# Regrouping 32-row blocks through DRAM instead of within SBUF, and another order of the first pair's loads and splits

## The chip, the cores and the metric

The kernel runs on one core of one Trainium2 chip. The metric is the time of one execution on the device in microseconds, the median of several runs. The engines are called as in the profile: PE is TensorE (matmuls; PEld its weight loads), DVE is VectorE, ACT is ScalarE, POOL is GpSimd, SP is SyncE, which here only issues DMAs.

## The reference

One layer of a hybrid encoder on x of 1 x 512 x 1024 in float32: an RMS norm, one wide input projection, two token mixers, a gated merge, an output projection and the residual.

```python
h = rmsnorm(x, norm_w)
proj = einsum('bsd,de->bse', h, w_in) + b_in
(mq, mk, mv, mi, mf, mo, mz, sq, sk, sv, sz, gates) = split(proj)
# A) mLSTM, 4 heads of 256, on conv+silu of mq, mk; y_m = rmsnorm(hm) * sigmoid(mo) * silu(mz)
# B) stick-breaking attention, 8 heads of 128, strictly causal:
#    A[t,s] = sigmoid(z_ts) * prod_{s<j<t} (1 - sigmoid(z_tj));  y_s = (A v) * silu(sz)
merged = g_m * (y_m @ w_proj_m) + g_s * (y_s @ w_proj_s)
out = x + merged @ w_out
```

## The kernel before

Every float32 operand of a matmul is split into a high and a low half in the matmul's own type (`wh` and `wl` for weights: a copy on ACT, a subtraction on DVE, or, where a unit is marked `by_dma`, a negated copy on ACT and an accumulating DMA issued by POOL), and each product is three matmuls (lines 94 to 96).

The dense work is a list of units, and the main loop runs over them: in step c it moves the result of unit c-1 out of PSUM (`evac`), runs what is due in step c (`later`; `defer(n, fn)` puts something n steps ahead), loads and splits the weights of the units ahead, issues the first half of unit c's matmuls, lets each active attention head take one step of its generator (up to its next `yield`), and issues the second half. In the steps of `REST` the heads do not advance. All of this is an order written by hand; each engine works through its own queue strictly in that order. A tile has a tag with a fixed number of buffers; a new tile waits until its buffer's last readers have finished. Tag A has four buffers, which the `ay`, `a_all` and `ty` tiles, `hz`, the first pair's `X` and `Y` and the token blocks of x share.

Units 0 to 3 make the first attention set's q (`first_mm`). Units 4 to 17 and 18 to 31 are two Strassen pairs (`Pair`, `Half`): seven products of two half units each instead of eight, with sums of the quarters of the weights (`X`, `Z`, `V`, `Y`, made by `t1` to `t4`; `t3` adds V to Y by a DMA of POOL) and of the quarters of h (`form_sum` on DVE over the copies `h32`, which `x_32` makes on ACT; `form_split` splits them on ACT and DVE). Half units take half the time of the later units. From unit E = 32 on come z of set 0, q, k and z of set 1, and then the gates and the mLSTM groups. The heads of set 0 and set 1 (`SbSet.head`) and the four mLSTM heads (`MPair.head`) run beside them.

Three places turn a matrix of 128-column blocks round. VectorE transposes 32 x 32 blocks, and DMAs then regroup blocks of 32 rows:
- `SbSet.turn` writes q or k transposed in blocks to `ty`; `move`, one step later, regroups it into `tz` by 16 DMAs of 32 KB, eight on SP's queue and eight on POOL's (line 441); `weight` then scales `tz` for q.
- `SbSet.head` writes the attention weights in blocks to `ay` and regroups them into `az` by 16 DMAs of 40 KB on SP's queue, eight in one step and eight in the next (line 542); `turn` splits `az` into `ath` and `atl` some steps later.
- `MPair.head` regroups `ht` into `hz` by 16 DMAs of 32 KB on SP's queue (line 874).

Of the kernel before, what the change touches and what calls it, by code (L numbers as in the profile page):

```python
# [8 lines left out]
F32 = mybir.dt.float32  # L9
# [28 lines left out]
def tile_hybrid_layer(  # L38
# [16 lines left out]
    nc = tc.nc  # L55
# [3 lines left out]
    def pool(name, bufs=1, **k):  # L59
        return ctx.enter_context(tc.tile_pool(name=name, bufs=bufs, **k))  # L60
# [6 lines left out]
    dp = pool("dp", space=bass.MemoryType.DRAM)  # L67
# [9 lines left out]
    def blk(tag, dt=F32, shape=(512,), name=None, p=128):  # L77

        where = mp if tag in MISC else sp
        return where.tile([p] + list(shape), dt, name=name or tag, tag=tag, bufs=BUFS[tag])  # L80
# [51 lines left out]
    units = []  # L132
# [72 lines left out]
    def defer(n, fn):  # L205
        later.setdefault(now[0] + n, []).append(fn)
# [78 lines left out]
    def x_scale(tb):  # L285
        x_norm(tb)
        x_mul(tb)
# [16 lines left out]
    def x_mul(tb):  # L304
        nc.vector.tensor_scalar(x_t[tb], x_t[tb], x_r[tb], None, op0=OP.mult)
# [3 lines left out]
    def x_tp(tb, g):  # L309
        tp = x_ps[tb, g] = att_ps()  # L310
        for j in range(4):
            kt = g * 4 + j
            nc.tensor.transpose(tp[:, j * 128:(j + 1) * 128], x_t[tb][:, kt * 128:(kt + 1) * 128], ident)

    def x_hh(tb, g):
        ks = slice(4 * g, 4 * g + 4)
        nc.vector.tensor_tensor(hh[:, ks, tb * 128:(tb + 1) * 128],
                                x_ps[tb, g].rearrange("p (k t) -> p k t", k=4),
                                nw_t[:, ks].unsqueeze(2).to_broadcast([128, 4, 128]), op=OP.mult)

    def x_hl(tb, *ks):
        ts = slice(tb * 128, (tb + 1) * 128)
        for k in ks:
            tp = x_ps[tb, k // 4][:, k % 4 * 128:k % 4 * 128 + 128]
            nc.vector.scalar_tensor_tensor(hl[:, k, ts], tp, nw_t[:, k:k + 1],
                                           hh[:, k, ts].bitcast(F32), op0=OP.mult, op1=OP.subtract)
# [3 lines left out]
    def x_32(tb, g):  # L330
        for k in range(4 * g, 4 * g + 4):
            at = tb // 2, k // 2
            if not at in h32:
                t = blk("vl", name="h32") if len(h32) < 5 else blk("vh", shape=(576,), name="h32")[:, 0:512]
                h32[at] = t.rearrange("p (k t) -> p k t", k=2)
            c = 128 * (tb % 2)
            nc.scalar.activation(h32[at][:, k % 2, c:c + 128], x_ps[tb, g][:, k % 4 * 128:k % 4 * 128 + 128],
                                 AF.Copy, scale=nw_t[:, k:k + 1])

    def x_turn(tb):  # L340
        for g in range(2):
            x_tp(tb, g)
            x_hh(tb, g)
            x_hl(tb, *range(4 * g, 4 * g + 4))
            if tb > 1:
                x_32(tb, g)
# [11 lines left out]
    class SbSet:  # L358
# [66 lines left out]
        def turn(self, name, g):  # L425

            ty = sp.tile([128, 8, TB, 32], F32, name="ty", tag="A", bufs=4)
            for tb in range(TB):  # L430
                nc.vector.transpose(ty[:, :, tb, :],  # L431
                                    self.raw[name][tb][:, 256 * g:256 * g + 256].rearrange("p (x j) -> p x j", j=32))

            def move():
                tz = blk("qk", F32, (2, 4, 128), name="tz")
                self.tz[name, g] = tz
                src = ty.rearrange("p (h b) i j -> p b h (i j)", h=2)
                for b in range(4):
                    for a in range(4):
                        q = nc.gpsimd if a % 2 else nc.sync  # L440
                        q.dma_start(tz[32 * b:32 * b + 32, :, a, :], src[32 * a:32 * a + 32, b])  # L441

            def weight():
                z = self.tz[name, g]
                nc.vector.tensor_scalar(z, z, qkw, None, op0=OP.mult)

            defer(1, move)
            if name == "q":
                defer(3 if self.s else 6, weight)
            if name == "q" and g == 0:  # L450
                defer(2, lambda: self.turn(name, 1))

# [11 lines left out]
        def head(self, h):  # L464
# [55 lines left out]
            ay = sp.tile([128, 4, 10, 32], F32, name="ay", tag="A", bufs=4)  # L520
# [16 lines left out]
                blocks(i)  # L537
            yield
            az = sp.tile([128, 4, 10, 32], F32, name="az", tag="P5", bufs=2)
            for b in range(4):  # L540
                for a in range(4):
                    nc.sync.dma_start(az[32 * a:32 * a + 32, b, :, :], ay[32 * b:32 * b + 32, a, :, :])  # L542
                if b == 1:
                    yield
            yield
            yield
            while not ("v", self.s) in done:
# [141 lines left out]
    class MPair:  # L689
# [85 lines left out]
        def head(self, h):  # L775
# [15 lines left out]
            for j in range(TB):  # L791
                lo = j * 128
                w = w_all[:, P_OFF[j]:P_OFF[j] + T - lo]
                for i in range(j, TB):
                    s = slice((i - j) * 128, (i - j + 1) * 128)
                    src = w[:, s] if i == j else rbc[:, i * 128:(i + 1) * 128]
# [53 lines left out]
            ht = sp.tile([128, 8, TB, 32], F32, name="ht", tag="A", bufs=4)  # L850
# [17 lines left out]
            turn(3)  # L868
            yield
            hz = sp.tile([128, 2, T], F32, name="hz", tag="A", bufs=4)  # L870
            src = ht.rearrange("p (d a) i j -> p a d (i j)", d=2)
            for a in range(4):
                for b in range(4):
                    nc.sync.dma_start(hz[32 * a:32 * a + 32, :, 128 * b:128 * b + 128],
                                      src[32 * b:32 * b + 32, a])
            yield
            yield
            for d in range(2):
                y = y_m[2 * hd + d].rearrange("p (i b j) -> p i b j", i=TB, b=4)
# [28 lines left out]
    def h_form(row, col):  # L908
        def sta(k, tb):
            c = slice(256 * row + 128 * tb, 256 * row + 128 * tb + 128)  # L910
            return hh[:, 4 * col + k, c], hl[:, 4 * col + k, c]
        return sta
# [49 lines left out]
    class Pair:  # L962

        def __init__(self, c1, c2, got1, got2):
            self.c = {1: c1, 2: c2}
            self.got = {1: got1, 2: got2}
            self.raw, self.bank, self.dst = {}, {}, {}
            self.sta = {1: h_form(0, 0), 2: h_form(0, 1), 6: s_form(6), 5: s_form(5),
                        7: s_form(7), 3: s_form(3), 4: h_form(1, 1)}
            b = self.base = len(units)  # L970
            for p in (1, 2, 6, 5, 7, 3, 4):
                for g in range(2):
                    units.append(Half(self, p, g))
            first = b == 4
            for g in range(2):
                if first:
                    plan = {"X": g, "Z": g, "V": g, "Y": 1}
                else:
                    plan = {"X": b - 8 + g, "Z": b - 8 + 6 * g, "V": b - 4 + g, "Y": b - 6 + g}
                for name, c in plan.items():  # L980
                    self.at(c, self.load, name, g)
                self.at(b + g - 2, self.t3, g)
                self.at(b + 1 + g, self.t2, g)
                self.at(b + 3 + g, self.t4, g)
                self.at(b + 4 + g, self.t1, g)
            self.at(b + 1, self.rows)

        def at(self, c, fn, *a):
# [75 lines left out]
    def at_unit(c, fn, *a):  # L1064
        later.setdefault(c, []).append(lambda: fn(*a))

    for g in range(2):
        at_unit(1 + g, units[4 + g].split)
    for f in (5, 7, 6):
        for i in range(2):  # L1070
            at_unit(2, form_sum, f, i)
    for f, c in ((6, 3), (5, 5), (7, 7), (3, 9)):
        for i in range(2):
            at_unit(c + i, form_split, f, i)
    for i in range(2):
        at_unit(8, form_sum, 3, i)

# [418 lines left out]
    for c in range(N):  # L1496
        now[0] = c
        if 0 < c < TB:
            ahead(c)
        if c and units[c - 1].slow:  # L1500
            units[c - 1].slow()
            ahead(c)
        due = later.pop(c, [])
        if c > n_proj - 9:
            ahead(c)
        if c:
            units[c - 1].evac()
        for fn in due:
            fn()
        ahead(c)  # L1510
        units[c].mm(0)
        if c == 0:
            x_tp(1, 0)
            x_tp(1, 1)
            x_hh(1, 0)
            x_hl(1, 0, 1, 2, 3)
            x_norm(2)
            x_mul(2)
            x_hh(1, 1)
            x_hl(1, 4, 5, 6, 7)  # L1520
            x_scale(3)
            for n in range(4):
                x_32(n // 2, n % 2)
        if c == 1:
            x_turn(2)
        for g in list(act):
            if c in REST:
                continue
            if next(g, "end") == "end":
                act.remove(g)  # L1530
        for e in list(pend):
            if c >= e[0] and e[2]():
                pend.remove(e)
                g = e[3]()
                next(g)
                act.append(g)
        units[c].mm(1)
        if c == 1:
            x_turn(3)
# [31 lines left out]
```

## Time and profile before

| | |
|---|---|
| median of 3 runs | 706.59 us (706.04 to 706.91) |
| profiled execution | 707.75 us, of which the span of its trace is 706.0 us |
| PE busy | 678.5 us, 96% |
| DVE, ACT, POOL busy | 490.1, 375.6, 151.8 us |
| mean granted clock of TensorE | 0.987 of full speed |
| moved by DMA | 101.52 MB, of which HBM read 69.37 MB, written 5.30 MB |
| issues for `az`, `hz`, `tz` | 128 and 64 on SP; 48 on SP and 48 on POOL |

A row of the timeline gives the start in us, the time taken, engine, line, operation, output and inputs by the program's names, and in square brackets how long the engine had been idle before it and what ended that. SPq and POOLq rows are issues of DMAs. A row with "x8" merges eight instructions that follow each other. A group's row gives its count, then busy time and the mean of one in ns, then the idle time before them. A row of DMA issues gives count, size and, for POOL, the median time from issue to landing.

### The profile page before, as it was taken

The page shows a single profiled execution, that of the slowest core. Times are in us where ns is not written, and L with a number is a line of the kernel's source. Part 1 is how long each engine was busy: PE and PEld are TensorE (multiplying, and loading weights), DVE is VectorE, ACT ScalarE, POOL GpSimd, SP SyncE. Part 2 cuts the span into 40 slices and gives each one's busy share as a digit, 9 for nine tenths or more (in the row PEclk, how much of TensorE's full clock was granted, in tenths as well). Part 3 has the DMA queues.
Part 4 walks back from the last instruction along what each step waited for, and adds up shares of the span by engine and source line. Part 5 has one row for each costly group of instructions (what it writes and reads, how often), then busy time and mean ns, then how long its engine had stood idle before and what let it go on. Part 6 is the DMA issues. An engine that isn't in the chain of part 4 may idle for free.

```text
span 706.0 us, 9541 instructions
## 1 busy us (share of the span) xinstructions
PE 678.5 (96%) x3114; PEld 562.3 (80%) x3114; DVE 490.1 (69%) x849; ACT 375.6 (53%) x705; POOL 151.8 (21%) x316
## 2 busy tenths in 40 slices
PE   7988999999949999999999999999999999999997
PEld 5876868888737888888887888888888888888786
DVE  6876687766466886698998446599733365545897
ACT  7656445765826554564445664444647452444361
POOL 4124327365634420130001031100001200111010
PEclk9998999999988999999999999999999999999999
DMA  7947947569643465525445414234332344989333
GB/s 244 303 101 208 234 132 180 143 163 221 154 120 103 107 188 178 156 57 144 102 97 146 134 60 120 77 104 133 106 103 70 90 123 139 307 189 225 112 78 102
DMA packets 128306, 101.52 MB, mean 144 GB/s; under 512 B 19786, under 2 KB 105188, under 8 KB 128256
## 3 DMA queue, kind: packets, MB, share of 16 engines
q1 hardware_dynamic: 121104, 83.48, 40.5%
q0 software_dynamic: 7008, 17.31, 12.8%
q8 instruction: 24, 0.39, 0.2%
q14 instruction: 26, 0.21, 0.1%
q10 hardware_dynamic: 144, 0.13, 0.1%
HBM read 69.37 MB, written 5.30 MB: 106 GB/s over the span
## 4 chain that ended last, share of the span: by engine, by line
PE 62%; DVE 9%; DMA 7%; issue 5%; ACT 4%; SPq 2%; POOL 0%; DVEq 0%; ACTq 0%; POOLq 0%
PE dps L96 17%; PE dps L94 17%; PE dps L95 17%; PE aps L95 2%; PE aps L96 2%; PE aps L94 2%; DMA wl<-stg 2%; DVE acc L724 2%; DMA stg<-in_w_in_dram 2%; DMA Y<-V 2%; SPq L542 2%; PE dps L955 2%; DVE wl L100 1%; PE aps L955 1%; DMA az<-ay 1%
## 5 line engine op out<-in xcount | busy, mean ns | idle before, releaser
L94 PE MATMUL dps<-hh,wh 128*128 128x512 f32 x448 | 176.5, 394 | 10.9 <-DVE kraw L387 10.4
L96 PE MATMUL dps<-hh,wl 128*128 128x512 f32 x448 | 175.4, 391 | 0.6 <-DVE wl L100 0.6
L95 PE MATMUL dps<-hl,wh 128*128 128x512 f32 x448 | 175.2, 391 | 0.0
L100 DVE TENSOR_TENSOR wl<-stg,wh 128x1024 fp32r<-128x1024 f32 x68 | 83.4, 1226 | 56.1 <-ACT wh L99 55.7
L94 PEld LDWEIGHTS dps<-hh,wh 128*128 128x128 f32 x448 | 84.7, 189 | 28.4 <-issue 10.8
L96 PEld LDWEIGHTS dps<-hh,wl 128*128 128x128 f32 x448 | 84.5, 189 | 19.1 <-DVE wl L100 1.1
L95 PEld LDWEIGHTS dps<-hl,wh 128*128 128x128 f32 x448 | 84.7, 189 | 16.8
L99 ACT ACTIVATE wh<-stg 128x1024 fp32r<-128x1024 f32 x68 | 71.6, 1052 | 29.4 <-PE dps L95 10.9
L506 DVE TENSOR_TENSOR_SCAN om<-om 128x512 f32<-128x512 f32 (+3 forms) x32 | 26.9, 839 | 19.3 <-POOL om L500 19.3
L94 PE MATMUL dps<-wh,hh 128*128 128x512 f32 x96 | 37.6, 392 | 1.3 <-DVE qraw L387 1.3
L727 ACT ACTIVATE tmp<-acc 128x512 f32<-128x512 f32 x16 | 10.1, 633 | 52.3 <-DVE acc L724 52.3
L95 PE MATMUL dps<-wl,hh 128*128 128x512 f32 x96 | 37.4, 390 | 0.0
L96 PE MATMUL dps<-wh,hl 128*128 128x512 f32 x96 | 37.4, 390 | 0.0
L724 DVE SCALAR_TENSOR_TENSOR acc<-tmp,vec,acc 128x511 f32<-128x511 f32 (+2 forms) x48 | 36.0, 750 | 1.7
L128 POOL DMA_DIRECT2D wl<-stg x16 | 14.3, 892 | 94.5 <-DVE yml L100 40.0
L126 ACT ACTIVATE wh<-stg 128x1024 fp32r<-128x1024 f32 x16 | 16.9, 1058 | 28.4 <-PE dps L95 16.9
L786 POOL TENSOR_SCALAR_AFFINE_SELECT w_all<-om 128x128 f32<-128x128 f32 x16 | 7.7, 514 | 108.3 <-DMA om<-rb_d 108.3
L441 POOL DMA_DIRECT2D tz<-ty x48 | 26.0, 570 | 12.7 <-DVE ty L431 6.6
L500 POOL TENSOR_SCALAR_AFFINE_SELECT om<-om 128x128 f32<-128x128 f32 x32 | 16.0, 506 | 58.3 <-ACT om L498 58.1
L96 PE MATMUL dps<-yh,wl 128*128 128x512 f32 x64 | 25.0, 391 | 0.6 <-DMA wl<-stg 0.6
L95 PE MATMUL dps<-yl,wh 128*128 128x512 f32 x64 | 24.9, 389 | 0.0
L94 PE MATMUL dps<-yh,wh 128*128 128x512 f32 x64 | 24.9, 389 | 0.0
(303 smaller groups left out, 1567.4 us busy)
## 6 DMA issues: line engine op xcount, KB each, us to landing
stg<-in_w_in_dram SPq DMA_DIRECT2D x71, 512.0 KB
wl<-stg POOLq DMA_DIRECT2D x16, 512.0 KB, 5.5
az<-ay SPq DMA_DIRECT2D x128, 40.0 KB
stg<-in_w_proj_s_dram SPq DMA_DIRECT2D x8, 512.0 KB
B<-in_w_out_dram SPq DMA_DIRECT2D x8, 512.0 KB
stg<-in_w_proj_m_dram SPq DMA_DIRECT2D x8, 512.0 KB
dst<-u POOLq DMA_DIRECT2D x12, 256.0 KB, 5.5
X<-in_w_in_dram SPq DMA_DIRECT2D x4, 512.0 KB
```

Of the source, the lines that this page charges most:

```text
L94: nc.tensor.matmul(ps, ah, bh, start=first, stop=False)
L95: nc.tensor.matmul(ps, ah, bl, start=False, stop=False)
L96: nc.tensor.matmul(ps, al, bh, start=False, stop=last)
L99: nc.scalar.activation(hi, src, AF.Copy)
L100: nc.vector.tensor_tensor(lo, src, hi.bitcast(F32), op=OP.subtract)
L126: nc.scalar.activation(self.wh, self.st, AF.Copy)
L128: nc.gpsimd.dma_start(out=self.wl, in_=self.st, accum_op=OP.add)
L441: q.dma_start(tz[32 * b:32 * b + 32, :, a, :], src[32 * a:32 * a + 32, b])
L500: nc.gpsimd.affine_select(out=om[:, ts], in_=om[:, ts], compare_op=OP.is_gt, fill=1.0, base=0, channel_multiplier=1, pattern=[[-1, 128]])
L506: nc.vector.tensor_tensor_scan(back, back, back, 1.0, op0=OP.mult, op1=OP.bypass)
L724: nc.vector.scalar_tensor_tensor(acc[:, j:], t[:, 0:T - j], cw(3 - j, ch), acc[:, j:], op0=OP.mult, op1=OP.add)
L955: nc.tensor.matmul(pr.bank[key, tb], a, w[:, i, :], start=begin and n == 0, stop=end and n == 2, skip_group_check=again)
```

## The change

The three regroupings go through a parking tile in DRAM. `tz`: four stores of 32 partitions each, and one step later (`back`) four loads, all on SP's queue; `weight` in set 1 moves from 3 to 4 steps after `turn`. `az`: one store of the whole `ay`, and one step later four loads. `hz`: four stores, and one step later four loads.

In the first pair, the eight weight loads go out as X0, Z0, V0 in step 0 and Y0, X1, V1, Y1, Z1 in step 1 (before, Z1 and V1 stood between X1 and Y1). The split of unit 5 moves from step 2 to step 1, behind the turning of token block 2 and ahead of that of block 3. The forms 5 and 7 are split one or two steps earlier.

```diff
             def move():
                 tz = blk("qk", F32, (2, 4, 128), name="tz")
                 self.tz[name, g] = tz
-                src = ty.rearrange("p (h b) i j -> p b h (i j)", h=2)
-                for b in range(4):
-                    for a in range(4):
-                        q = nc.gpsimd if a % 2 else nc.sync
-                        q.dma_start(tz[32 * b:32 * b + 32, :, a, :], src[32 * a:32 * a + 32, b])
+                park = dp.tile([32, 2, 4, 4, 128], F32, name="t_d", tag="t_d", bufs=3)
+                for a in range(4):
+                    nc.sync.dma_start(park[:, :, :, a].rearrange("i h b x -> i (h b) x"),
+                                      ty[32 * a:32 * a + 32].rearrange("i g n j -> i g (n j)"))
+
+                def back():
+                    for b in range(4):
+                        nc.sync.dma_start(tz[32 * b:32 * b + 32].rearrange("i h a x -> i h (a x)"),
+                                          park[:, :, b].rearrange("i h a x -> i h (a x)"))
+
+                defer(1, back)
...
             if name == "q":
-                defer(3 if self.s else 6, weight)
+                defer(4 if self.s else 6, weight)
...
             az = sp.tile([128, 4, 10, 32], F32, name="az", tag="P5", bufs=2)
-            for b in range(4):
-                for a in range(4):
-                    nc.sync.dma_start(az[32 * a:32 * a + 32, b, :, :], ay[32 * b:32 * b + 32, a, :, :])
-                if b == 1:
-                    yield
+            park = dp.tile([4, 32, 4, 320], F32, name="a_d", tag="a_d", bufs=3)
+            nc.sync.dma_start(park.rearrange("b i a x -> (b i) (a x)"), ay.rearrange("p a n j -> p (a n j)"))
+            yield
+            for a in range(4):
+                nc.sync.dma_start(az[32 * a:32 * a + 32].rearrange("i b n j -> i b (n j)"),
+                                  park[:, :, a].rearrange("b i x -> i b x"))
             yield
             yield
...
             hz = sp.tile([128, 2, T], F32, name="hz", tag="A", bufs=4)
-            src = ht.rearrange("p (d a) i j -> p a d (i j)", d=2)
+            park = dp.tile([32, 2, 4, 4, 128], F32, name="h_d", tag="h_d", bufs=2)
+            for b in range(4):
+                nc.sync.dma_start(park[:, :, :, b].rearrange("i d a x -> i (d a) x"),
+                                  ht[32 * b:32 * b + 32].rearrange("i g n j -> i g (n j)"))
+            yield
             for a in range(4):
-                for b in range(4):
-                    nc.sync.dma_start(hz[32 * a:32 * a + 32, :, 128 * b:128 * b + 128],
-                                      src[32 * b:32 * b + 32, a])
-            yield
+                nc.sync.dma_start(hz[32 * a:32 * a + 32], park[:, :, a].rearrange("i d b x -> i d (b x)"))
             yield
...
             first = b == 4
             for g in range(2):
-                if first:
-                    plan = {"X": g, "Z": g, "V": g, "Y": 1}
-                else:
+                if not first:
                     plan = {"X": b - 8 + g, "Z": b - 8 + 6 * g, "V": b - 4 + g, "Y": b - 6 + g}
...
+            if first:
+                for n, (name, g) in enumerate((("X", 0), ("Z", 0), ("V", 0), ("Y", 0), ("X", 1),
+                                               ("V", 1), ("Y", 1), ("Z", 1))):
+                    self.at(n // 3 if n < 4 else 1, self.load, name, g)
...
-    for g in range(2):
-        at_unit(1 + g, units[4 + g].split)
+    at_unit(1, units[4].split)
...
-    for f, c in ((6, 3), (5, 5), (7, 7), (3, 9)):
+    for f, c in ((6, (3, 4)), (5, (4, 5)), (7, (5, 6)), (3, (9, 10))):
         for i in range(2):
-            at_unit(c + i, form_split, f, i)
+            at_unit(c[i], form_split, f, i)
...
         if c == 1:
             x_turn(2)
+            units[5].split()
```

More of the change, by code (lines that the diff above doesn't have):

```diff
@@ L975, in __init__ @@
             for g in range(2):
-                if first:
-                    plan = {"X": g, "Z": g, "V": g, "Y": 1}
-                else:
+                if not first:
                     plan = {"X": b - 8 + g, "Z": b - 8 + 6 * g, "V": b - 4 + g, "Y": b - 6 + g}
-                for name, c in plan.items():
-                    self.at(c, self.load, name, g)
+                    for name, c in plan.items():
+                        self.at(c, self.load, name, g)
                 self.at(b + g - 2, self.t3, g)
```

## The prediction

> **What bounds the kernel now.** I read the first part of the page, then what TensorE waited for, then the clock by stretches, then the timeline of the engine each wait names.
>
> ```profile
> span 706.0 us, 9541 instructions
> PE 678.5 (96%) x3114; PEld 562.3 (80%) x3114; DVE 490.1 (69%) x849; ACT 375.6 (53%) x705; POOL 151.8 (21%) x316
> ...
> PE dps L94 <- DVE kraw L387: 10.4, 1, 10.4
> PE aps L955 <- DVE wl L100: 3.8, 3, 2.4
> PE dps L955 <- DMA wl<-X: 2.2, 1, 2.2
> ```
>
> TensorE is busy for 678.5 of 706.0 us, so the change adds and removes no matmul and can only move the other 27.5. Two thirds of that are these waits (columns: us in total, times, longest): one of 10.4 us where the z group of the second attention set starts, and two in the first Strassen pair.
>
> ```profile
> 56.00:60.00 4.00, 2.38 (x6) 1.91 (x7) 3.42 (x5) 1.70 (x3) 0.43 (x2) 0.58 0.39 96
> 60.00:64.00 4.00, 4.00 (x12) 3.14 (x11) 1.89 (x3) 3.90 (x13) 0.90 (x2) 0.57 0.97 307
> 64.00:68.00 4.00, 4.00 (x20) 3.27 (x19) 2.27 (x2) 3.31 (x12) 1.14 (x2) 1.00 0.75 258
> ...
> 211.00:215.00 4.00, 2.16 (x5) 1.80 (x6) 4.00 (x7) 2.08 (x11) 0.33 (x2) 0.50 0.85 239
> 215.00:219.00 4.00, 4.00 (x14) 3.14 (x14) 2.04 (x4) 1.97 (x7) 2.11 (x3) 0.74 0.12 32
> ```
>
> Busy time by stretches (TensorE first; third from the right is the granted clock). Each long gap is followed by a half clock: 12 matmuls in 4 us against 20 at full clock. Six in 2.38 us instead of 12, then 12 instead of 20, is 14 x 0.2 = 2.8 us lost behind the first pair's gap; 5 instead of 11 and 14 instead of 20 is 2.4 us behind the 10.4 us one.
>
> ```profile
> 196.73 0.29 DVE L507 TENSOR_TENSOR a_all<-a_all,om 128x128 f32<-128x128 f32 x1
> 202.62 1.42 DVE L431 STREAM_TRANSPOSE ty<-qraw 128x256 f32<-128x256 f32 x4 [5.59 <-DMA az<-ay]
> ...
> 212.01 2.48 DVE L387 TENSOR_TENSOR kraw<-dps,brow 128x512 f32<-128x512 f32 x4
> 212.84 0.76 PE L94 MATMUL dps<-hh,wh 128*128 128x512 f32 x1 [10.37 <-DVE kraw L387]
> 188.76 5.91 SPq L542 DMA_DIRECT2D az<-ay  x8
> ...
> 195.82 5.40 SPq L542 DMA_DIRECT2D az<-ay  x8
> ```
>
> TensorE needs the four banks that `kraw` empties. VectorE gets there late: it stands 5.59 us at `ty`, whose buffer (tag A) still holds an `ay` that 16 transfers are reading, eight issued from 188.76 and eight, one step later, from 195.82 to 201.22.
>
> **The change, part by part: regrouping.** *az.* Sixteen transfers (11.3 us of SP) become one store and, a step later, four loads; at the same 0.7 us each, some 3.5. What matters is who reads `ay`: now the store alone, at the place of 188.76. So `ty` waits for a landing at 188.76 plus that of a 640 KB transfer. The nearest rows are these:
>
> ```profile
> wl<-stg POOLq DMA_DIRECT2D x16, 512.0 KB, 5.5
> Y<-V POOLq DMA_DIRECT2D x4, 512.0 KB, 8.8
> 702.86 0.37 ACTq L1313 DMA_DIRECT2D out_dram<-xr  x1
> ...
> L441 POOL DMA_DIRECT2D tz<-ty x48 | 26.0, 570 | 12.7 <-DVE ty L431 6.6
> ```
>
> The third is a 128 KB store to DRAM at the very end; with the span's end at 706.0 it took 3.1 us from the start of its issue. At 3.1 the store lands at 191.9, at 5.5 at 194.3, at 8.8 at 197.6; VectorE arrives at 197.02. I take 5.5 (nearest in size): no wait is left, gain 5.59; at 8.8 it is 5.0. Late next is VectorE itself: from `ty` to `kraw` it takes 212.01 - 202.62 = 9.39 us without a break, so `kraw` starts at 197.02 + 9.39 = 206.4 and TensorE, 0.83 later as before, at 207.2. The gap shrinks from 10.37 to 4.8: **-5.6 us**. It is still long; I keep the 2.4 us of half clock.
>
> *ty to tz.* Eight issues on SP and eight on POOL become four stores and, one unit later, four loads, all on SP. POOL loses 48 issues, 26.0 us by the fourth row, but TensorE's waits above name none of them: 0. On SP the loads must wait until the stores have landed, and everything behind them on that queue, weight loads above all, waits too; that is the rival below. With `weight` moved from 3 to 4 units, `q` of the second set is scaled in the unit that starts its first head, one VectorE operation over 128 x 1024, ahead of that head in the same queue: 0, and at most the 1.2 us that such an operation takes below (37.91), at a place where TensorE has no long gap.
>
> *hz.* Four stores, a step, four loads for 16 transfers, 64 issues to 32 in all; the product still follows after the same number of steps, and no wait of TensorE stands in that part: 0. If loads came late there, the product would wait on VectorE, which is idle for 31% of the span.
>
> **The first pair.**
>
> ```profile
> 23.13 1.06 ACT L938 ACTIVATE wh<-X 128x1024 fp32r<-128x1024 f32 x1 [2.48 <-DMA X<-in_w_in_dram]
> 25.05 2.32 ACT L337 ACTIVATE h<-aps,nw_t 128x128 f32<-128x128 f32 x8
> ...
> 29.74 1.14 ACT L337 ACTIVATE h<-aps,nw_t 128x128 f32<-128x128 f32 x4 [0.61 <-DVE hl L325]
> 30.76 1.08 ACT L938 ACTIVATE wh<-X 128x1024 fp32r<-128x1024 f32 x1
> 38.14 1.06 ACT L99 ACTIVATE wh<-Z 128x1024 fp32r<-128x1024 f32 x1 [1.84 <-PE dps L955]
> 28.27 0.87 POOL L1000 DMA_DIRECT2D Y<-V  x1 [1.75 <-DMA Y<-in_w_in_dram]
> 33.07 0.85 POOL L940 DMA_DIRECT2D wl<-X  x1 [3.93 <-ACT wl L939]
> 39.84 0.86 POOL L1000 DMA_DIRECT2D Y<-V  x1 [5.92 <-DVE form L906]
> 30.40 3.70 DVE L897 TENSOR_TENSOR h<-h,h 128x512 f32<-128x512 f32 x6
> 37.91 1.22 DVE L1004 TENSOR_TENSOR X<-X,Y 128x1024 f32<-128x1024 f32 x1
> 44.31 1.23 DVE L1004 TENSOR_TENSOR X<-X,Y 128x1024 f32<-128x1024 f32 x1 [3.44 <-issue]
> 47.06 1.23 DVE L100 TENSOR_TENSOR wl<-X,wh 128x1024 fp32r<-128x1024 f32 x1 [0.92 <-ACT wh L99]
> 56.35 1.22 DVE L100 TENSOR_TENSOR wl<-X,wh 128x1024 fp32r<-128x1024 f32 x1
> 40.53 0.50 PE L955 MATMUL dps<-wl,hh 128*128 128x512 f32 x1 [2.20 <-DMA wl<-X]
> 57.62 0.80 PE L955 MATMUL aps<-wl,form 128*128 128x512 f32 x1 [2.43 <-DVE wl L100]
> ```
>
> The split of unit 5 goes ahead of the copies of token block 3 on ACT, and its `wl<-X` ahead of both `Y<-V` on POOL. Issued at 33.07 it lands at 40.5; some 2 us earlier, the 2.20 us wait at 40.53 goes. But that is not where the pair gets its time: TensorE only arrives earlier at 57.62, where it waits for VectorE's `wl` of 56.35. VectorE works from 30.40 to 57.57 with two idle stretches, 3.44 + 0.92 = 4.36. The 3.44 ends with the second `Y<-V` (39.84 plus a landing), which the new order of loads brings forward: V and Y of the second half no longer stand behind Z. So VectorE could end 4.36 earlier, less what its start is delayed.
>
> And it is delayed: ACT, free at 27.4, must now wait for the second X before it copies block 3, which the sums at 30.40 read. That X landed by 30.76, since ACT took it then without waiting. Between the first X (23.13) and the first Y (28.27) lie three loads, 1.7 each; one more gives 30.0, and at the earliest 27.4 costs nothing. I take 29.2. Then two copies at 0.95 apart (1.9), the first six of eight pieces of block 3 (1.7), and the sums at 32.8 instead of 30.4: 2.4 late. The gain is 4.36 - 2.4 = **-2.0 us**; with X at 27.4 the sums are 0.6 late, gain 3.8; at 30.76, 4.0 late, gain 0.3. `f5` and `f7`, split earlier, stay ahead of 56.35 in VectorE's queue either way: 0. Z's second half, now last of the eight loads, lands when Y's did (by 39.84) instead of before 38.14: at most 1.7 on ACT, which has nothing else until TensorE ends the unit; without that cover 1.7. The first `Y<-V`, behind `wl<-X` on POOL, starts at 32 instead of 28.27 and lands by 40.9 (8.8), when VectorE reaches its reader (37.91 + 2.4 + 0.6). I keep the 2.8 us of half clock.
>
> **Sum.** -5.6 - 2.0 = -7.6. The profiled execution took 707.75 us (span 706.0 and 1.75 around it), 1.16 above the median of the runs, 706.59: it would take 700.1, and the median **699.0**.
>
> **The rivals.** *The clock stays up.* With gaps of some 3 and 4.8 us broken up or ending sooner, the granted clock need not fall: back come 2.4 us at the z group, and of the pair's 2.8 some 1.0 (between 0 and 2.8, nearer the lower end, since VectorE's chain behind 56.35 sets the pace there): 699.0 - 3.4 = 695.6. For it: 40.53's gap of 2.20 us left no half clock. Against: 57.62's 2.43 us did.
> [...]
>
> *The wait at `ty` stays.* If what frees its buffer is not the store but another reader, only the pair's 2.0 us come: 704.6. The row at 202.62 names `az<-ay`, whose last transfer was issued just before; but releasers are inferred.
>
> *Slower: SP stands behind its own stores.*
>
> ```profile
> 103.35 10.45 SPq L441 DMA_DIRECT2D tz<-ty  x16
> 113.90 5.71 SPq L119 DMA_DIRECT2D stg<-in_w_in_dram  x3
> ...
> 122.17 1.04 ACT L99 ACTIVATE wh<-stg 128x1024 fp32r<-128x1024 f32 x1
> 126.63 0.39 PE L94 MATMUL dps<-hh,wh 128*128 128x512 f32 x1
> 188.21 3.51 DMA stg<-in_w_in_dram
> ```
>
> Where `q` of the first set is turned, units are half as long, so both pairs of stores and loads follow each other directly. 16 issues take 10.45 us now and then, but two landings L come in between: the first weight load goes out at 113.9 + 2L. TensorE needs it at 126.63, less 3.5 (landing), 1.05 (ACT) and 1.2 (VectorE): by 120.9, so L decides at 3.5. The 128 KB store above gives 3.1 with its issue, 2.8 without. At L = 5.5 the load is 4.0 late, and a half clock's 2.4 follows: 705.4; at 8.8 it is 10.6 late: 712.0.
>
> **How the numbers follow.** Likeliest, 0.50: 699.0, its own range 697 to 701.5 from the bounds of the second X and of the store. Clock stays up 0.18: 695.6. Wait stays 0.15: 704.6. SP behind its stores 0.09: 705 to 712. The other 0.08: only part of the z group's gap, near 702. The range 695.0 to 704.6 leaves out the slow case and the tails. A measurement of this kernel tells 0.2% (1.4 us) from no change: faster 0.84 (two thirds of "wait stays" with it), same 0.08, slower 0.08.
>
> **What the next profile should show.** `ty` of the second set's `q` without an idle stretch; a gap at the z group's first matmul of 4 to 5 us; no wait of TensorE for `wl<-X`; ACT waiting 1 to 2.5 us for the second X, and the sums of `h` 2 to 3 us later; the pair's wait for `wl` ending near 55.5. I am wrong if `ty` still waits, if the sums push the pair's wait past 57, or if the first weight load behind the turned `q` of the first set comes too late for 126.63.

## The result, and the profile after

The change makes the kernel faster: 699.21 us (697.80 to 699.99, 4 runs) against 706.72 (706.04 to 706.91, 4 runs), a ratio of 0.9893 with a 95% interval of 0.9876 to 0.9910. On another chip the ratio was 0.9870 (0.9852 to 0.9888; `c2_after_again` below). The forecast was 699.0 us, 0.989 of the time before. The profiled execution took 699.28 us, with a span of 697.5, 8.5 us shorter than before.

From the head of the page after:

```profile
PE 677.6 (97%) x3114; PEld 560.4 (80%) x3114; DVE 489.6 (70%) x849; ACT 374.9 (54%) x705; POOL 133.0 (19%) x268
...
HBM read 79.85 MB, written 15.79 MB: 137 GB/s over the span
```

The work is the same: 3114 matmuls, VectorE and ACT as busy as before. POOL has lost the issues of `tz`. Some 10.5 MB more are written to HBM and read back (5.30 and 69.37 MB before), and no wait of TensorE in this profile names these transfers. So the 8.5 us are idle time and half clock of TensorE (0.995 of full speed granted over the span, 0.987 before). Its waits after (us in total, times, longest):

```profile
PE aps L963 <- DVE wl L100: 4.1, 5, 1.8
PE dps L94 <- DVE kraw L387: 4.1, 1, 4.1
...
PE aps L481 <- DVE dst L419: 1.3, 2, 0.8
```

The wait for `kraw` fell from 10.4 to 4.1, the 2.2 us wait for `wl<-X` in the first pair is gone, and a wait that did not exist before has come, in `L481`. The waits for VectorE's `wl` in the pairs (`aps L963`, `L955` before) have not fallen in sum, 4.1 us against 3.8; they stand at other places. The three places one by one, in the timeline (start, time taken, engine; SPq rows are issues of DMAs).

*The z group of the second set.*

```profile
194.97 0.29 DVE L513 TENSOR_TENSOR a_all<-a_all,om 128x128 f32<-128x128 f32 x1
195.18 1.42 DVE L431 STREAM_TRANSPOSE ty<-qraw 128x256 f32<-128x256 f32 x4
...
204.57 1.88 DVE L387 TENSOR_TENSOR kraw<-dps,brow 128x512 f32<-128x512 f32 x3
...
205.40 0.77 PE L94 MATMUL dps<-hh,wh 128*128 128x512 f32 x1 [4.09 <-DVE kraw L387]
```

`ty` follows the row above it without an idle stretch, where it stood 5.59 us before. VectorE then works 204.57 - 195.18 = 9.39 us up to `kraw`, to the hundredth what it took before, and TensorE starts 0.83 behind that, as before.

*The first pair.*

```profile
22.53 1.06 ACT L946 ACTIVATE wh<-X 128x1024 fp32r<-128x1024 f32 x1 [2.19 <-DMA X<-in_w_in_dram]
28.58 1.06 ACT L946 ACTIVATE wh<-X 128x1024 fp32r<-128x1024 f32 x1 [1.98 <-DMA X<-in_w_in_dram]
...
32.16 3.70 DVE L905 TENSOR_TENSOR h<-h,h 128x512 f32<-128x512 f32 x6 [2.68 <-ACT h L337]
...
53.57 1.23 DVE L100 TENSOR_TENSOR wl<-X,wh 128x1024 fp32r<-128x1024 f32 x1
54.85 0.50 PE L963 MATMUL aps<-wl,form 128*128 128x512 f32 x1 [1.82 <-DVE wl L100]
58.40 0.50 PE L963 MATMUL aps<-wl,form 128*128 128x512 f32 x1 [0.53 <-DVE wl L100]
62.43 0.50 PE L963 MATMUL dps<-wl,form 128*128 128x512 f32 x1 [0.76 <-DVE wl L100]
100.67 0.50 PE L963 MATMUL aps<-wl,form 128*128 128x512 f32 x1 [0.56 <-DVE wl L100]
```

ACT waits 1.98 us for the second `X`, the sums of `h` start late, and VectorE has no idle stretch between 32.16 and 57: the 4.36 us of before are gone. TensorE resumes at 54.85 instead of 57.62, of which 0.60 is a run that began earlier (first copy of `X` at 22.53 instead of 23.13). The last row is a matmul of the second pair; the same one in the kernel before:

```profile
104.03 0.50 PE L955 MATMUL aps<-wl,form 128*128 128x512 f32 x1 [0.55 <-DVE wl L100]
```

*Where the first set's q is turned.* This is the place of the slower rival.

```profile
99.53 2.66 SPq L439 DMA_DIRECT2D t_d<-ty  x4
...
104.02 2.50 SPq L444 DMA_DIRECT2D tz<-t_d  x4
106.56 2.60 SPq L439 DMA_DIRECT2D t_d<-ty  x4
...
111.20 2.83 SPq L444 DMA_DIRECT2D tz<-t_d  x4
114.08 3.72 SPq L119 DMA_DIRECT2D stg<-in_w_in_dram  x3
119.52 1.06 ACT L99 ACTIVATE wh<-stg 128x1024 fp32r<-128x1024 f32 x1 [2.21 <-DMA stg<-in_w_in_dram]
124.18 1.06 ACT L99 ACTIVATE wh<-stg 128x1024 fp32r<-128x1024 f32 x1 [2.81 <-DMA stg<-in_w_in_dram]
...
131.23 0.39 PE L96 MATMUL dps<-hh,wl 128*128 128x512 f32 x1
132.42 0.33 PE L481 MATMUL aps<-ident,dst 128*128 128x128 f32 x1 [0.80 <-DVE dst L419]
...
133.50 0.48 PE L94 MATMUL dps<-hh,wh 128*128 128x512 f32 x1
```

SP stands from 102.19 to 104.02 and from 109.16 to 111.20 until its own stores have landed (its waits name `t_d<-ty` there), 1.83 and 2.04 us. The weight loads behind go out at 114.08 (113.90 before), although TensorE is 3.4 us earlier here (100.67 against 104.03). ACT waits for them twice, VectorE behind ACT scales `dst` late, and around the four transposes of `L481` 2.27 us pass from the last matmul ahead of them to the first behind (133.50 - 131.23).

### The profile page after: what moved, and what is told of

It reads as the page before. It is cut to its first block, busy times and chain, and to the rows that moved or that the text cites. A ratio compares the mean times of both kernels' runs of the same rounds, so it can differ in the third digit from the quotient of the medians.

```text
span 697.5 us, 9279 instructions
## 1 busy us (share of the span) xinstructions
PE 677.6 (97%) x3114; PEld 560.4 (80%) x3114; DVE 489.6 (70%) x849; ACT 374.9 (54%) x705; POOL 133.0 (19%) x268
## 4 chain that ended last, share of the span: by engine, by line
PE 67%; DMA 7%; DVE 6%; issue 4%; ACT 3%; SPq 2%; POOL 0%; DVEq 0%; ACTq 0%; POOLq 0%
PE dps L94 19%; PE dps L95 19%; PE dps L96 19%; PE aps L95 3%; PE aps L96 3%; PE aps L94 3%; DMA stg<-in_w_in_dram 2%; DVE acc L731 2%; DMA Y<-V 2%; DMA t_d<-ty 1%; ACT sqj L404 1%; DMA wl<-stg 1%; DVE wl L100 1%; PE aps L840 1%; PE aps L842 1%
## 5 line engine op out<-in xcount | busy, mean ns | idle before, releaser
L504 ACT ACTIVATE om<-aps,rq 128x512 f32<-128x512 f32 (+3 forms) x32 | 16.9, 528 | 12.7 <-PE aps L96 11.7
```

Source lines behind the costliest of these rows:

```text
L504: nc.scalar.activation(om[:, 0:n], zp, AF.Sigmoid, scale=rn[:, h:h + 1])
```

## The experiments

The times before on the chips used were 708.0 (the `a` runs), 708.45 (`b`), 708.73 (`c`) and 708.02 us (`d`), so kernels of different letters are compared by their ratios to before. Edits are against the changed kernel unless said otherwise.

| kernel | median us | ratio, 95% interval |
|---|---|---|
| changed kernel, first and second chip | 699.21; 698.78 | 0.9893 (0.9876 to 0.9910); 0.9870 (0.9852 to 0.9888) |
| a1_regroup_only | 702.43 | 0.9921 (0.9906 to 0.9935) |
| a2_pair_only | 704.05 | 0.9943 (0.9926 to 0.9959) |
| a3_tz_in_sbuf | 698.42 | 0.9868 (0.9853 to 0.9883) |
| a4_az_store_late | 705.15 | 0.9961 (0.9948 to 0.9974) |
| b1_split5_back | 700.09 | 0.9891 (0.9864 to 0.9919) |
| b2_loads_back | 698.90 | 0.9868 (0.9845 to 0.9892) |
| b3_heads_rest | 693.77 | 0.9791 (0.9763 to 0.9820) |
| b4 and c4, pair order | 700.42; 699.60 | 0.9907 (0.9872 to 0.9941); 0.9888 (0.9865 to 0.9910) |
| c1_tz_and_rest | 694.79 | 0.9815 (0.9794 to 0.9836) |
| d1_tz_set0_and_rest | 692.89 | 0.9792 (0.9779 to 0.9806) |

**The two halves of the change, each alone.** First the regroupings, with the first pair as before:

```diff
-                if not first:
+                if first:
+                    plan = {"X": g, "Z": g, "V": g, "Y": 1}
+                else:
...
-                for n, (name, g) in enumerate((("X", 0), ("Z", 0), ("V", 0), ("Y", 0), ("X", 1),
-                                               ("V", 1), ("Y", 1), ("Z", 1))):
-                    self.at(n // 3 if n < 4 else 1, self.load, name, g)
...
-    at_unit(1, units[4].split)
+    for g in range(2):
+        at_unit(1 + g, units[4 + g].split)
-    for f, c in ((6, (3, 4)), (5, (4, 5)), (7, (5, 6)), (3, (9, 10))):
+    for f, c in ((6, 3), (5, 5), (7, 7), (3, 9)):
...
         if c == 1:
             x_turn(2)
-            units[5].split()
```

> Regrouping through DRAM as changed, first pair (loads, split of unit 5, splits of the forms) as before. Theory: the gap before the second set's z group falls from 10.4 to 4 to 5 us and keeps its half clock, while the first pair keeps its wait for wl<-X (2.2 us), its gap of 2.9 us and the half clock behind it: 706.7 - 6 + about 1 for SP standing behind its stores = 701 to 702.5. Rival, most of the gain is the first pair's: 704 or more.

Then the first pair alone, by the reverse of this edit on the kernel before, with all regroupings as they were:

> First pair as changed, all three regroupings as before. Theory: no wait for wl<-X, the clock stays up in the pair, some of that turns into new waits: 706.7 - 2.2 - 1.1 = 703 to 704; the gap before the z group stays near 10 us and its ty waits 5 to 6 us for az<-ay. Rival, the pair carries most: 701 or less.

The times came out at the upper end of what was expected: 708.0 to 702.43 is 5.6 us, and 708.0 to 704.05 is 4.0. The clock in the pair did not come as expected: it stayed up behind the 2.43 us wait of the first kernel and fell to half behind the shorter wait, 1.82 or 1.83 us, of the second (0.995 and 0.988 granted over the profiled executions). Together the gains are 9.6 us, 1.36%; the whole change gives 1.07% and 1.30% in its two measurements, so the halves add within what the intervals can tell. The traces, first of the regroupings alone:

```profile
40.42 0.80 PE L963 MATMUL dps<-wl,hh 128*128 128x512 f32 x1 [2.56 <-DMA wl<-X]
58.91 0.50 PE L963 MATMUL aps<-wl,form 128*128 128x512 f32 x1 [2.43 <-DVE wl L100]
...
199.59 1.42 DVE L431 STREAM_TRANSPOSE ty<-qraw 128x256 f32<-128x256 f32 x4
```

and of the pair alone:

```profile
200.71 1.42 DVE L431 STREAM_TRANSPOSE ty<-qraw 128x256 f32<-128x256 f32 x4 [5.70 <-DMA az<-ay]
```

Each half removes its own waits and leaves the other's: the pair's 2.56 and 2.43 stand in the first, the 5.70 at `ty` in the second, which waits for no `wl<-X`.

**Is it the store of `ay` that frees `ty`, and not the smaller number of transfers?** The same transfers, with the store of `ay` one step later:

```diff
             az = sp.tile([128, 4, 10, 32], F32, name="az", tag="P5", bufs=2)
             park = dp.tile([4, 32, 4, 320], F32, name="a_d", tag="a_d", bufs=3)
+            yield
             nc.sync.dma_start(park.rearrange("b i a x -> (b i) (a x)"), ay.rearrange("p a n j -> p (a n j)"))
             yield
             for a in range(4):
...
-            yield
             yield
```

> The changed kernel with the store of ay one step later and the loads one more (the same number of steps until az is used). Theory (what counts is the step at which ay is last read): ty waits again for the store, 3 to 5 us, the gap before the z group grows to 7 to 9 us: 702 to 704. Rival (what counts is the number of issues on SP): ty does not wait, 699 to 700.

```profile
195.94 0.57 SPq L548 DMA_DIRECT2D a_d<-ay  x1
...
201.55 1.42 DVE L431 STREAM_TRANSPOSE ty<-qraw 128x256 f32<-128x256 f32 x4 [6.15 <-DMA a_d<-ay]
```

705.15 us, above the 702 to 704 expected: of the change's 1.07 to 1.30% only 0.39% is left, with as few transfers as in the changed kernel. `ty` waits as it did before the change, now for the single store. So the gain at the z group is not that 16 transfers became 5; it is that the last reader of `ay` is issued one step earlier. The row also gives the number that the prediction had to bound: 201.55 - 195.94 = 5.61 us from the issue of the 640 KB store to the release of its source (5.5 was taken).

**Does SP stand behind its own stores?** `tz` by 16 transfers within SBUF as before, all else as changed:

```diff
-                park = dp.tile([32, 2, 4, 4, 128], F32, name="t_d", tag="t_d", bufs=3)
-                for a in range(4):
-                    nc.sync.dma_start(park[:, :, :, a].rearrange("i h b x -> i (h b) x"),
...
-                defer(1, back)
+                src = ty.rearrange("p (h b) i j -> p b h (i j)", h=2)
+                for b in range(4):
+                    for a in range(4):
+                        q = nc.gpsimd if a % 2 else nc.sync
+                        q.dma_start(tz[32 * b:32 * b + 32, :, a, :], src[32 * a:32 * a + 32, b])
-                defer(4 if self.s else 6, weight)
+                defer(3 if self.s else 6, weight)
```

> The changed kernel with tz regrouped by 16 transfers on SP and POOL as before (az and hz through DRAM). Theory (SP stands behind its own stores where q of the first set is turned): ACT no longer waits for stg near 119 to 124 us and TensorE not for the scaled k at 131 to 133 us, 1.5 us; 699.2 - 1.5 = 697.0 to 698.2. Rival, that wait has another cause (the shift of everything against the loads): 699 to 700, the wait stays.

```profile
120.03 1.05 ACT L99 ACTIVATE wh<-stg 128x1024 fp32r<-128x1024 f32 x1
...
132.37 0.39 PE L96 MATMUL dps<-hh,wl 128*128 128x512 f32 x1
...
132.96 0.48 PE L94 MATMUL dps<-hh,wh 128*128 128x512 f32 x1
```

The waits of ACT and of `L481` (here L475) are gone: from the last matmul ahead of the transposes to the first behind it are 0.59 us instead of 2.27. So the parking of `tz` costs 1.7 us at this place. The profiled execution of this run began later (first copy of `X` at 23.59 instead of 22.53); counted from there, TensorE is past the transposes after 132.96 - 23.59 = 109.37 us instead of 133.50 - 22.53 = 110.97. The times do not settle it: the ratio, 0.9868, is under the changed kernel's 0.9893 and equal to its 0.9870 on the second chip.

**Which edit of the first pair does it?** First the split of unit 5 back in step 2, with the new loads:

```diff
-    at_unit(1, units[4].split)
+    for g in range(2):
+        at_unit(1 + g, units[4 + g].split)
...
-            units[5].split()
```

> The changed kernel with the split of unit 5 back in step 2 (loads and forms in the new order). Theory: the 2 us wait for wl<-X returns, ACT no longer waits for the second X and the sums come 2 us earlier; but ACT's copies of the first product then end 2 us later, so VectorE's wl of unit 10 comes about 1 us later than in the changed kernel: 0.9 to 1.5 us above it, ratio to the kernel before 0.991. Rival (ACT's wait for the second X is the larger cost): 1 us below it, 0.988.

Then the old order of loads, with the early split:

```diff
-                if not first:
+                if first:
+                    plan = {"X": g, "Z": g, "V": g, "Y": 1}
+                else:
...
-                for n, (name, g) in enumerate((("X", 0), ("Z", 0), ("V", 0), ("Y", 0), ("X", 1),
-                                               ("V", 1), ("Y", 1), ("Z", 1))):
-                    self.at(n // 3 if n < 4 else 1, self.load, name, g)
```

> The changed kernel with the old order of the eight loads (Z and V of the second half between X and Y). Theory of the prediction, that the early Y<-V is what ends VectorE's idle 3.44 us: the second Y<-V lands at 43 to 44 again and VectorE's wl of unit 10 starts up to 1 us later: up to 1 us above the changed kernel, ratio 0.989 to 0.991. Rival, the order of loads is worth the pair's whole 2 us: 0.992.

By time the first is undecided (0.9891, between the two expectations, its interval holding both), and the second shows no loss at all (0.9868). The traces decide, by VectorE's `wl` for which TensorE waits longest in the pair, counted from the first copy of `X` in the same run. First the split back, then the loads back:

```profile
23.06 1.06 ACT L946 ACTIVATE wh<-X 128x1024 fp32r<-128x1024 f32 x1 [2.45 <-DMA X<-in_w_in_dram]
...
44.41 1.23 DVE L1014 TENSOR_TENSOR X<-X,Y 128x1024 f32<-128x1024 f32 x1 [1.75 <-DMA Y<-V]
55.37 1.22 DVE L100 TENSOR_TENSOR wl<-X,wh 128x1024 fp32r<-128x1024 f32 x1
```

```profile
23.45 1.06 ACT L946 ACTIVATE wh<-X 128x1024 fp32r<-128x1024 f32 x1 [2.60 <-DMA X<-in_w_in_dram]
...
44.99 1.22 DVE L1012 TENSOR_TENSOR X<-X,Y 128x1024 f32<-128x1024 f32 x1
54.80 1.22 DVE L100 TENSOR_TENSOR wl<-X,wh 128x1024 fp32r<-128x1024 f32 x1
```

Before it was 56.35 - 23.13 = 33.22 us. New loads with the late split: 55.37 - 23.06 = 32.31. Old loads with the early split: 54.80 - 23.45 = 31.35. Both: 53.57 - 22.53 = 31.04. Both single edits stand beside the early splits of the forms 5 and 7, which no kernel takes back alone, so these differences are not the price of one edit each. With the early split the second `X<-X,Y` waits for no `Y<-V` even in the old order of loads, and 1.9 of the 2.2 us are there. The new order with the late split does not bring this operation forward: it starts 44.41 - 23.06 = 21.35 us after the first copy, where it was 44.31 - 23.13 = 21.18 before. Its `Y<-V` was issued earlier (37.30 - 23.06 = 14.24 us after the first copy, 39.84 - 23.13 = 16.71 before) but took 7.0 us to land instead of 4.4, and TensorE's wait for `wl<-X` is back as well. What this kernel gains, 0.9 us, comes behind `X<-X,Y`: from there to `wl` VectorE takes 55.37 - 44.41 = 10.96 us instead of 56.35 - 44.31 = 12.04, with one `form` operation in the stretch (45.55) instead of three (45.45, 49.33, 54.54); the others now fill its idle time ahead. So what this trace shows is the forms' gain, not one of the order of loads.

**What is left at the z group.** 4.09 us of gap remain since VectorE has 9.39 us of work between `ty` and `kraw`. The attention heads put most of it there; they rest in the steps of `REST`. Two of these rests, one step earlier:

```diff
-REST = {E + n for n in (4, 8, 11, 12, 48)}
+REST = {E + n for n in (4, 8, 10, 11, 48)}
```

> The changed kernel with the heads resting in steps E+10 and E+11 instead of E+11 and E+12, so that VectorE's head work (atl, ay, scans, about 6 us) comes behind kraw. Theory, that VectorE's own queue sets what is left of the gap: it falls from 4.1 us to under 1.5 us and the clock stays up there, 3 to 5 us: 694.5 to 696.5, ratio 0.983 to 0.986. Rival (something else holds kraw, or the work comes back as a wait later): 698.5 or more.

```profile
197.01 0.50 PE L95 MATMUL dps<-wl,hh 128*128 128x512 f32 x1 [0.78 <-DMA wl<-stg]
...
196.23 1.42 DVE L431 STREAM_TRANSPOSE ty<-qraw 128x256 f32<-128x256 f32 x4
...
199.80 2.11 DVE L387 TENSOR_TENSOR kraw<-dps,brow 128x512 f32<-128x512 f32 x3
```

0.9791, more than expected: from `ty` to `kraw` VectorE now takes 3.57 us, TensorE waits only 0.78 us for a weight, and the half clock behind the gap is gone with the gap (0.998 granted over the profiled execution, 0.995 in the changed kernel's).

**The waits at units 11 and 12 of the pair.** The last two sums of `h` and their splits later, and the second `t4` one step later:

```diff
-                self.at(b + 3 + g, self.t4, g)
+                self.at(b + 3 + (2 * g if first else g), self.t4, g)
-    for f, c in ((6, (3, 4)), (5, (4, 5)), (7, (5, 6)), (3, (9, 10))):
+    for f, c in ((6, (3, 4)), (5, (4, 5)), (7, (5, 6)), (3, (11, 12))):
-        at_unit(8, form_sum, 3, i)
+        at_unit(10, form_sum, 3, i)
```

> The changed kernel with the second t4 one step and the last two sums of h two steps later (and the splits of form 3 with them), behind the weight split of unit 10 on VectorE. Theory (VectorE's queue sets the pair's wait at unit 10): wl of unit 10 comes 2.3 us earlier, that wait of about 2 us goes, of which 1 us returns at units 11 and 12, where ACT's queue sets the pace: 1 us below the changed kernel, ratio 0.987 to 0.989. Rival (ACT sets the pace already): no change, 0.9893.

No gain: 0.9907. One execution, the profiled one, took 1748.5 us, so the kernel was run again for its trace, beside the changed kernel itself:

> The changed kernel with the second `t4` of the first pair one step later and the last two sums of `h` and their splits later (two places further), once more, for a trace of it. Theory: the waits of TensorE for `wl` at units 11 and 12 come from the earlier splits ahead in VectorE's queue and should shrink from 1.7 together to below 0.5; a gain of 1 to 2 us. Rival, which the first times speak for: they only move, since VectorE has no idle time left between 33 and 57 us, and some other unit of the pair waits instead: within 0.5 us of the changed kernel.

> The changed kernel as it is, on this chip, as the measure for the two others. 0.988 to 0.991 of the kernel before. In the clock: if the half clock in the first pair depends on where the gaps fall and not on the order of the work, this run may show it (some 1.7 us for each 3.4 us stretch) although the first profile of this kernel did not; if the new order of the pair is what keeps the clock up, it does not show it.

```profile
22.73 1.06 ACT L946 ACTIVATE wh<-X 128x1024 fp32r<-128x1024 f32 x1 [2.27 <-DMA X<-in_w_in_dram]
...
52.84 1.23 DVE L100 TENSOR_TENSOR wl<-X,wh 128x1024 fp32r<-128x1024 f32 x1 [1.18 <-ACT wh L99]
...
54.12 0.50 PE L963 MATMUL aps<-wl,form 128*128 128x512 f32 x1 [0.76 <-DVE wl L100]
...
62.44 0.50 PE L963 MATMUL dps<-wl,form 128*128 128x512 f32 x1 [0.50 <-DVE wl L100]
```

As the rival said, there is no gain: 699.60 beside 698.78 us, a little more than the 0.5 us that it allowed, with ratios whose intervals overlap (0.9888 and 0.9870). The 1.82 us wait fell to 0.76, and others stand further on: 0.73 us for ACT's `wh` at 57.66, 0.77 at 58.92 and 0.50 at 62.44, where TensorE is 62.44 - 22.73 = 39.71 us after the first copy, against 62.43 - 22.53 = 39.90 in the changed kernel. But the reason that the rival gave, a VectorE without idle time, does not hold here. VectorE now stands idle ahead of `wl`, 1.18 us at 52.84 and 1.18 again at 57.64, until ACT has copied `wh`, and ACT can do that only when VectorE's `X<-X,V` is done. With the other work gone from between them, it is this chain from VectorE to ACT and back that TensorE waits for, as the rival on record before the first of the two runs had it (ACT sets the pace).

**Both improvements together.** `tz` in SBUF (a3) and the heads' rest (b3):

> The changed kernel with `tz` regrouped by 16 transfers within SBUF as before and with the heads resting in steps E+10 and E+11. My theory: the two losses are at different places (the stores of `tz` hold up the weight loads near 114, the heads hold up VectorE near 196), so both gains come: the waits at L481 near 132 and at `kraw` near 205 are both gone. Beside the changed kernel on the same chip 6 to 8 us less (7 from the heads, 0 to 1 from `tz`), 0.977 to 0.979 of the kernel before. Rival: the transfers of the second set's `tz` on POOL's queue collide with the heads that now run a step later, and some of the z group's gap comes back: no better than the resting heads alone, 0.979 to 0.982.

The rival's outcome: 0.9815, no better than the rest alone.

```profile
203.62 1.42 DVE L431 STREAM_TRANSPOSE ty<-qraw 128x256 f32<-128x256 f32 x4 [2.78 <-DMA tz<-ty]
...
216.62 0.39 PE L95 MATMUL aps<-atl,vh 128*128 128x256 f32 x1 [0.99 <-DVE atl L100]
218.44 0.33 PE L475 MATMUL aps<-ident,kraw 128*128 128x128 f32 x1 [0.79 <-DVE kraw L419]
219.22 0.47 PE L475 MATMUL aps<-ident,kraw 128*128 128x128 f32 x1 [0.46 <-DVE kraw L419]
```

Nothing is lost near 132 any more. But the mechanism is another than I had written: in the second set the 16 transfers read `ty` for so long that VectorE waits 2.78 us to write the next one, and TensorE pays 2.24 for it near 217, and more through the clock, which fell to half there (0.59 granted from 218 to 222 us). So with the heads' rest moved, the route through DRAM is worth something for `tz` too, in the second set. Hence the last kernel, DRAM for the second set and SBUF for the first, with the heads' rest moved:

```diff
             def move():
+                if not self.s:
+                    src = ty.rearrange("p (h b) i j -> p b h (i j)", h=2)
+                    for b in range(4):
+                        for a in range(4):
+                            q = nc.gpsimd if a % 2 else nc.sync
+                            q.dma_start(tz[32 * b:32 * b + 32, :, a, :], src[32 * a:32 * a + 32, b])
+                    return
                 park = dp.tile([32, 2, 4, 4, 128], F32, name="t_d", tag="t_d", bufs=3)
```

> The heads resting in steps E+10 and E+11, `tz` of the first set within SBUF as before the change, `tz` of the second set through DRAM as after it. My theory: the DRAM route frees `ty` early and pays where the second set is turned; it holds SP's queue and costs where the first set is turned, with units half as long. Then neither the waits at L481 near 132 (1.3 us) nor VectorE's idle stretch of 2.8 us ahead of the second `ty` near 203 nor the waits behind it near 217 (2.2 us) are there: 1 to 1.5 us less than with the resting heads alone, 692 to 693 us, 0.975 to 0.979 of the kernel before. Rival: the two places do not add, and some other wait takes up the 1.3 us, as the resting heads with all of `tz` in SBUF did: 0.979 to 0.982.

```profile
132.23 0.60 PE L488 MATMUL aps<-ident,dst 128*128 128x128 f32 x4
...
200.84 1.42 DVE L431 STREAM_TRANSPOSE ty<-qraw 128x256 f32<-128x256 f32 x4
```

Neither wait is there (of those near 217 one of 0.45 us is left), and its time is the shortest here, 692.89 us (692.60 to 693.23), 0.8 to 1.0% under the changed kernel by the ratios. By ratio, 0.9792, it is not to be told from the rest alone (0.9791), whose interval is twice as wide: the trace shows the waits near 132 gone, but the times do not show a gain from it.

## Why the prediction was right, point by point

The time came out 0.2 us above the forecast, and the two main terms held, each shown by a kernel of its own. Four sizes inside were off and nearly cancelled; that the sum came this close is luck.

1. *Regrouping of `az`, forecast -5.6 us: -6.3 in the trace* (10.37 to 4.09). The mechanism is shown by `a1` and, from the other side, by `a4`. The steps (no wait at `ty`, 9.39 us of VectorE behind it, 0.83 to TensorE) came as written, and the landing taken, 5.5 us, was measured as 5.61 (`a4`). The other 0.7: VectorE now reaches `ty` 201.31 - 195.18 = 6.1 us before TensorE stops, where it was 202.47 - 197.02 = 5.45.

2. *The half clock at the z group, kept: right.* The changed kernel, by stretches, read as those of before:

```profile
56.00:60.00 4.00, 3.47 (x16) 2.54 (x15) 2.45 (x3) 3.88 (x12) 3.84 (x5) 1.00 1.01 302
...
203.00:207.00 4.00, 1.60 (x4) 1.34 (x5) 4.00 (x7) 1.55 (x9) 0.00 (x0) 0.58 0.80 233
207.00:211.00 4.00, 4.00 (x12) 3.14 (x11) 2.61 (x6) 2.50 (x10) 2.43 (x4) 0.57 0.72 204
```

12 matmuls instead of 20 and 4 instead of 8 are 12 x 0.2 = 2.4 us, the size written for before. It left only when `b3` took the gap itself away.

3. *The half clock in the pair, kept: wrong in this run, and worth less than its 2.8 us.* The first of these three rows has 16 matmuls at full clock. That is half of the rival "the clock stays up". But TensorE then meets the waits of 0.53 and 0.76 us behind VectorE; in `a3`, whose clock fell behind the same wait, there is none at the first of these places and 0.27 us at the second. From the pair's wait to the matmul at 100.67 the lead over before grew only from 2.77 (57.62 - 54.85) to 3.36 (104.03 - 100.67): 0.6 us. I had given 1.0 for it in that rival, for this reason. Kernels with the same pair show still less: the matmul at 62.43 comes 39.90 us after the first copy here and 40.09 in `c1`, both at full clock, and 39.96 to 40.21 in `a3`, `b3` and `d1`, at half clock.

4. *The pair, forecast -2.0: -2.2* (33.22 to 31.04 from the first copy). The sums of `h` came 2.36 later (32.16 less 29.80, which is 30.40 with the 0.60 of the earlier start), against 2.4 forecast. But the cause that I gave for the 4.36 us of idle time, the order of the loads, is not shown: `b2` has no such idle time in the old order, with the early split, and in `b1` the new order without it leaves `X<-X,Y` where it was (21.35 us after the first copy, 21.18 before). The step that failed is "which the new order of loads brings forward". Why the early split brings `Y<-V` forward (issued 36.78 - 23.45 = 13.33 us after the first copy in `b2`, 16.71 before) stays open.

5. *`tz`, forecast 0: +1.7 us*, shown by `a3`. The place and mechanism were those of the slower rival, and its working for SP held: 114.08 follows from 99.53, 10.59 of issues and two landings of 1.83 and 2.04, far under the 3.5 from which it was to decide. What failed was the need behind it: I took 3.5 us for the landing of the first load, and ACT took that load 119.52 - 114.08 = 5.4 us after its issue, and I looked only at TensorE's matmul at 126.63, which indeed did not wait. The one that waited was at 132.42, behind VectorE. The step that failed was to price the late load by its first reader alone; the slack ran out at a later one.

6. *`hz` and POOL's issues, costed at nothing: no wait of TensorE names either* in the profile after. Neither was tried alone.

Of the 8.5 us between the spans, 3.4 come up to 100.67, 7.4 up to the z group's first matmul (212.84 to 205.40: 6.3 of gap, less 2.2 given back in between, of which 1.7 is point 5), and the rest behind it, from small waits that no step of mine names and that I did not trace.

## What to carry to other kernels

Where a buffer's reuse stalls an engine, ask which transfer reads it last and at which step that one is issued; fewer and larger transfers helped only where they moved this forward (`a4` has as few, and `ty` waits 6.15 us), and the same route cost time where its second half made a queue wait with urgent loads behind it (1.7 us, by `a3`). The same edit can be right in one place and wrong in another where the steps have another length (`tz` through DRAM costs those 1.7 us in the first set; in the second, without it, VectorE waits 2.78 us in `c1`), so try it place by place. And where two engines work on one chain in turn, reordering the queue of one moved TensorE's waits (`c4`: 1.82 us became 0.76, with 0.73, 0.77 and 0.50 further on); taking other work out of the chain's way removed one (`b3`: the 4.09 us for `kraw`).

## What the runs showed of the hardware that I had not expected

The same gap does not always bring the half clock. TensorE's wait at unit 10 of the first pair is 1.82 or 1.83 us in ten of these profiles. In four of them (the changed kernel twice, `b1`, `c1`) the clock stayed at 1.00 behind it, and in six (`a2`, `a3`, `a4`, `b2`, `b3`, `d1`) it fell to half, as here in `a3`, whose gap ended at 56.22:

```profile
56.00:60.00 4.00, 3.78 (x10) 3.03 (x11) 3.15 (x5) 2.60 (x5) 3.93 (x4) 0.57 0.67 215
```

against 16 matmuls at 1.00 in the stretch from 56 to 60 us shown under point 2. The order of the work is the same there; what differs is when the gap falls. In these profiles the times at which the granted clock changes lie whole multiples of one step apart. In the kernel before they are 56.62, 63.45, 206.81 and 217.05, so 6.83, 143.36 and 10.24 us apart: 2, 42 and 3 times 3.413 us, a third of the last. In the changed kernel they are 203.65 and 210.48, 6.83 or two steps apart. In `a3` the clock fell at 56.24, and one step ahead of that is 52.82: the whole gap lay between them, in a stretch with 2.09 us of idle time in all. In the changed kernel 53.47, 44 steps ahead of 203.65, cut the gap, and the stretch behind it held 1.38 us. Over all ten, the fullest stretch around this gap held 1.79 to 2.09 us of idle time where the clock fell and 1.21 to 1.46 where it did not. The runs show no sharp limit between them: in `a1`, behind its 2.43 us wait, a stretch with 1.82 us left the clock up.

For a forecast that means a short gap's half clock is a chance and not a sum, here six in ten, and that its price was under the time it halved where VectorE set the pace: by point 3, 0.6 us of lead in the pair for 2.8.
